# Storing the last four slabs of a 90-degree rotation in 16 KB instead of 8 KB packets

## The chip, the cores and the metric

One core of one Trainium2 chip. The metric is device time in microseconds (us), the median of several executions. A profile's span is the part of it between the first and the last instruction that the profile shows; it is about 1.8 us shorter than the time.

A ratio of two kernels is the mean time of one kernel's fast runs over the mean of the other's fast runs of the same rounds, so it is not quite the ratio of the medians quoted beside it.

## The reference

```python
def setup_inputs():
    batch, c, h, w = 32, 3, 256, 256
    return {"x": np.random.randn(batch, c, h, w).astype(np.float32)}

def reference(x):
    return np.rot90(x, k=-1, axes=(-2, -1)).astype(np.float32)
```

There are 96 images of 256 x 256 fp32 values, each turned by 90 degrees. That is 25.17 MB in and 25.17 MB out, without arithmetic.

## The kernel before

The images are handled in 12 slabs of 8 images, 2 MiB each. A slab is a tile of 128 partitions with 2 x 2048 values. VectorE turns it with two transposes of 128x2048 (STREAM_TRANSPOSE in the trace, 3.83 to 3.95 us each in the means of the page's groups); the rest of the rotation lies in the access patterns. With a right result a slab has long contiguous rows on one side only: if a partition holds 16 rows of the input (16 KB) it ends with twice 8 rows of the output (8 KB), or the other way round.

Before the change, slabs 1 to 8 are loaded in 16 KB rows and slabs 0, 9, 10 and 11 ("plain") in 8 KB rows. All are stored in 8 KB rows. Every DMA is issued from one engine, SyncE. A DMA of 1 MiB is spread over 16 DMA engines, and each row is one packet: the page's 5888 packets are 5248 rows (128 of slab 1, stored in two pieces, count twice) and 40 x 16 completion packets.

```python
    plain = (0, last - 2, last - 1, last)
    # ... views of the rows of x and out: ld8_v, st_v in 8 rows, ld16_v in 16 rows ...
    for n in range(n_slabs):
        for i in range(I):                                   # I = 2
            if n in plain:
                nc.sync.dma_start(out=units[n][:, i], in_=ld8_v[n][:, i])
            else:
                nc.sync.dma_start(out=units[n][i::I].rearrange("p i f -> p (i f)"), in_=ld16_v[n, i])

    for n in range(n_slabs):
        t_in, t_out = units[n], units[n - 1] if n else turned0        # turned0 lies in PSUM
        if n in plain:
            for i in range(I):
                src = t_in[:, i].rearrange("p (r g c) -> p c r g", r=RO, c=RO)
                dst = t_out[:, i].rearrange("p (c g r) -> p c r g", c=RO, r=RO)
                nc.vector.transpose(out=dst[:, :, ::-1, ::-1], in_=src)
        else:
            # ... two transposes, one per half of the rows of out ...
        # slab 1 is stored in three transfers, slabs 2 and 3 in two, the others in one:
        # ...
        elif n:
            nc.sync.dma_start(out=st_v[n], in_=t_out)

    for i in range(I):
        nc.scalar.copy(out=units[last][:, i], in_=turned0[:, i])
    nc.sync.dma_start(out=st_v[0], in_=units[last])
```

Slab n is turned into the tile that slab n - 1 came from; slab 0 waits in PSUM, and ScalarE copies it out at the end. So the order of stores is slab 1, 2, ... 11, and then 0.

## Time and profile before

| | before |
|---|---|
| time, median of 3 | 123.53 us (123.49 to 123.58) |
| span | 121.8 us |
| VectorE busy | 92.7 us, 76% |
| DMA packets, share of 16 engines | 5888, 98.1% |

The first line is the chain of work that ended last, by engine; then come the costliest groups: line, engine, operation, target and source, count, busy time in us, mean ns of one, and the idle time before them.

```profile
DVE 41%; issue 33%; DMA 4%; DVEq 3%; ACT 2%
...
L80 DVE STREAM_TRANSPOSE u<-u 128x2048 f32<-128x2048 f32 x16 | 62.4, 3945 | 0.3
L74 DVE STREAM_TRANSPOSE u<-u 128x2048 f32<-128x2048 f32 x6 | 22.8, 3931 | 0.0
L74 DVE STREAM_TRANSPOSE turned<-u 128x2048 f32<-128x2048 f32 x2 | 7.6, 3828 | 5.6 <-DMA u<-in_x_dram 5.6
```

VectorE (DVE) heads the chain and has almost no idle time once it has started. Both look like a bound.

### The profile page before, as it was taken

Reading aid. Unit: us, or ns where it says so; the run is one execution under the profiler, and the core shown is the slowest. Engines: PE = TensorE matmul, PEld = TensorE weight load, DVE = VectorE, ACT = ScalarE, POOL = GpSimd, SP = SyncE. Lnnn points to the kernel's source line nnn. Section 1 sums busy time; section 2 is a strip of 40 time slices with the busy share of each in tenths; the row PEclk is TensorE's granted clock in tenths of the full one; section 3 lists DMA queues with packets and bytes.
Section 4 is the critical chain, followed back from the end, with each engine's and each line's share of the span. In section 5 each row is a group of like instructions: output and inputs, shape, how many; then the busy total and the mean of one; then the engine's idle time right before and its main releaser. Section 6 shows DMA issues by size and latency. Waiting matters only on the chain.

```text
span 121.8 us, 140 instructions
## 1 busy us (share of the span) xinstructions
DVE 92.7 (76%) x24; ACT 5.0 (4%) x3; POOL 0.2 (0%) x4
## 2 busy tenths in 40 slices
DVE  0199999999999999999999999999999930000000
ACT  0000000000000000000300000000000660000000
POOL 0000000000000000000000000000000000000000
DMA  3999999999999999999999999999999999999995
GB/s 86 425 436 430 430 430 430 430 430 430 430 430 430 430 430 403 430 422 420 420 397 429 430 425 425 430 425 430 428 430 430 428 430 430 425 425 428 425 430 218
DMA packets 5888, 50.33 MB, mean 413 GB/s; under 512 B 640, under 2 KB 768, under 8 KB 896
## 3 DMA queue, kind: packets, MB, share of 16 engines
q1 hardware_dynamic: 5888, 50.33, 98.1%
HBM read 25.17 MB, written 25.17 MB: 413 GB/s over the span
## 4 chain that ended last, share of the span: by engine, by line
DVE 41%; issue 33%; DMA 4%; DVEq 3%; ACT 2%
DVE u L80 31%; DVE turned L74 6%; DMA u<-in_x_dram 4%; DVE u L74 4%; DVEq L120 3%; ACT u L93 2%
## 5 line engine op out<-in xcount | busy, mean ns | idle before, releaser
L80 DVE STREAM_TRANSPOSE u<-u 128x2048 f32<-128x2048 f32 x16 | 62.4, 3945 | 0.3
L74 DVE STREAM_TRANSPOSE u<-u 128x2048 f32<-128x2048 f32 x6 | 22.8, 3931 | 0.0
L74 DVE STREAM_TRANSPOSE turned<-u 128x2048 f32<-128x2048 f32 x2 | 7.6, 3828 | 5.6 <-DMA u<-in_x_dram 5.6
L93 ACT COPY u<-turned 128x2048 f32<-128x2048 f32 x2 | 3.7, 1865 | 35.8 <-DVE u L74 35.8
L93 ACT ACT_TABLE_LOAD x1 | 1.3, 1283 | 59.7 <-DMA u<-in_x_dram 59.7
L109 POOL MEMSET const-bfloat16-1.0<- 128x1 bf16 x1 | 0.1, 101 | 0.0
L109 POOL MEMSET const-uint8-127<- 128x1 uint8 x1 | 0.1, 101 | 0.0
L109 POOL MEMSET const-float32-0.0<- 128x1 f32 x1 | 0.1, 98 | 0.2 <-issue 0.2
L109 POOL MEMSET const-float32-1.0<- 128x1 f32 x1 | 0.1, 98 | 0.0
## 6 DMA issues: line engine op xcount, KB each, us to landing
u<-in_x_dram SPq DMA_DIRECT2D x24, 1024.0 KB, 19.6
out_dram<-u SPq DMA_DIRECT2D x9, 2048.0 KB, 22.8
out_dram<-u SPq DMA_DIRECT2D x5, 1024.0 KB, 17.4
out_dram<-u SPq DMA_DIRECT2D x1, 896.0 KB, 17.5
out_dram<-u SPq DMA_DIRECT2D x1, 128.0 KB, 18.0
```

The costliest lines, as they stand in the source:

```text
L74: nc.vector.transpose(out=dst[:, :, ::-1, ::-1], in_=src)
L80: nc.vector.transpose(out=dst[:, cs], in_=src[:, cs])
L93: nc.scalar.copy(out=units[last][:, i], in_=turned0[:, i])
L109: nc = _bacc.Bacc("TRN2", target_bir_lowering=False, num_devices=1)
L120: with _tile.TileContext(nc) as tc:
```

## The change

Its intent is fewer and longer packets in the stores. The four slabs that are loaded in 8 KB rows are turned the other way, so that a partition holds 16 rows of out, and are stored as two transfers of 64 rows of 16 KB each. To keep the number of transfers, two slabs are loaded, and two stored, in one transfer instead of two.

```diff
     for n in range(n_slabs):
+        if n in (last - 2, last - 1):
+            ld = nc.sync.dma_start(out=units[n], in_=ld_short[n])
+            continue
# ... cut ...
+    def store(n, t, i):
+        if n in long_st:
+            return nc.sync.dma_start(out=st_long[n, i], in_=t[i::I].rearrange("p i f -> p (i f)"))
+        return nc.sync.dma_start(out=st_short[n][:, i], in_=t[:, i])
# ... cut ...
-        if n in plain:
-            for i in range(I):
-                src = t_in[:, i].rearrange("p (r g c) -> p c r g", r=RO, c=RO)
-                dst = t_out[:, i].rearrange("p (c g r) -> p c r g", c=RO, r=RO)
-                nc.vector.transpose(out=dst[:, :, ::-1, ::-1], in_=src)
+        if n in long_st:
+            src = t_in.rearrange("p i (r g c) -> p c r g i", r=RS, c=RL)
+            dst = t_out.rearrange("p i f -> p (i f)").rearrange("p (c k r) -> p c r k", c=RL, r=RS)[:, :, ::-1, ::-1]
+            pieces = 2
+            for h in range(pieces):
+                cs = slice(h * RL // pieces, (h + 1) * RL // pieces)
+                nc.vector.transpose(out=dst[:, cs], in_=src[:, cs])
# ... cut: slabs 2 and 3 stored in one transfer each, slabs 9 to 11 in two each ...
-    nc.sync.dma_start(out=st_v[0], in_=units[last])
+    for i in range(I):
+        store(0, units[last], i)
```

More of the change, by code (lines that the diff above doesn't have):

```diff
@@ L40, with short, long @@
     P = nc.NUM_PARTITIONS
-    RI, RO = 16, 8
-    K = H // RI
+    RL, RS = 16, 8
     I = 2
-    Q = P // (K * I)
+    Q = P * RS // H
     n_slabs = B * C // (Q * I)
     last = n_slabs - 1
-    plain = (0, last - 2, last - 1, last)
-    F = RO * W
+    F = RS * W
+    long_st = (0, last - 2, last - 1, last)
     rows_in = x.rearrange("b c h w -> (b c h) w")
     rows_out = out.rearrange("b c h w -> (b c h) w")
-    ld8_v = rows_in.rearrange("(n i p r) w -> n p i (r w)", i=I, p=P, r=RO)
-    ld16_v = rows_in.rearrange("(n i m r) w -> n i m (r w)", i=I, m=Q * K, r=RI)
-    st_v = rows_out.rearrange("(n i p c) w -> n p i (c w)", i=I, p=P, c=RO)
+    def short(rows):
+        return rows.rearrange("(n i p r) w -> n p i (r w)", i=I, p=P, r=RS)
+    def long(rows):
+        return rows.rearrange("(n i m r) w -> n i m (r w)", i=I, m=P // I, r=RL)
+    ld_short, ld_long, st_short, st_long = short(rows_in), long(rows_in), short(rows_out), long(rows_out)
     pools = [ctx.enter_context(tc.tile_pool(name=f"unit{u}", bufs=1)) for u in range(n_slabs)]
@@ L61 @@
     for n in range(n_slabs):
+        if n in (last - 2, last - 1):
+            ld = nc.sync.dma_start(out=units[n], in_=ld_short[n])
+            continue
         for i in range(I):
-            if n in plain:
-                nc.sync.dma_start(out=units[n][:, i], in_=ld8_v[n][:, i])
-            else:
-                nc.sync.dma_start(out=units[n][i::I].rearrange("p i f -> p (i f)"), in_=ld16_v[n, i])
+            if n in long_st:
+                ld = nc.sync.dma_start(out=units[n][:, i], in_=ld_short[n][:, i])
+            else:
+                ld = nc.sync.dma_start(out=units[n][i::I].rearrange("p i f -> p (i f)"), in_=ld_long[n, i])
@@ L68 @@
+    def store(n, t, i):
+        if n in long_st:
+            return nc.sync.dma_start(out=st_long[n, i], in_=t[i::I].rearrange("p i f -> p (i f)"))
+        return nc.sync.dma_start(out=st_short[n][:, i], in_=t[:, i])
     for n in range(n_slabs):
         t_in, t_out = units[n], units[n - 1] if n else turned0
-        if n in plain:
-            for i in range(I):
-                src = t_in[:, i].rearrange("p (r g c) -> p c r g", r=RO, c=RO)
-                dst = t_out[:, i].rearrange("p (c g r) -> p c r g", c=RO, r=RO)
-                nc.vector.transpose(out=dst[:, :, ::-1, ::-1], in_=src)
-        else:
-            src = t_in.rearrange("p i f -> p (i f)").rearrange("p (r g c) -> p c r g", r=RI, c=RO)
-            dst = t_out.rearrange("p i (c k r) -> p c r k i", c=RO, r=RI)[:, :, ::-1, ::-1, :]
-            for h in range(2):
-                cs = slice(h * RO // 2, (h + 1) * RO // 2)
-                nc.vector.transpose(out=dst[:, cs], in_=src[:, cs])
@@ L82 @@
-        if n == 1:
-            nc.sync.dma_start(out=st_v[n][:, 0, :W], in_=t_out[:, 0, :W])
-            nc.sync.dma_start(out=st_v[n][:, 0, W:], in_=t_out[:, 0, W:])
-            nc.sync.dma_start(out=st_v[n][:, 1], in_=t_out[:, 1])
-        elif n in (2, 3):
-            for i in range(I):
-                nc.sync.dma_start(out=st_v[n][:, i], in_=t_out[:, i])
-        elif n:
-            nc.sync.dma_start(out=st_v[n], in_=t_out)
+        if n in long_st:
+            src = t_in.rearrange("p i (r g c) -> p c r g i", r=RS, c=RL)
[4 more added lines that the diff above has]
+                nc.vector.transpose(out=dst[:, cs], in_=src[:, cs])
+        else:
+            src = t_in.rearrange("p i f -> p (i f)").rearrange("p (r g c) -> p c r g", r=RL, c=RS)
+            dst = t_out.rearrange("p i (c k r) -> p c r k i", c=RS, r=RL)[:, :, ::-1, ::-1, :]
+            for h in range(2):
+                cs = slice(h * RS // 2, (h + 1) * RS // 2)
+                nc.vector.transpose(out=dst[:, cs], in_=src[:, cs])
@@ L92 @@
+        if n in range(2, last - 2):
+            nc.sync.dma_start(out=st_short[n], in_=t_out)
+        elif n:
+            for i in range(I):
+                if (n, i) == (1, 0):
+                    nc.sync.dma_start(out=st_short[n][:, 0, :W], in_=t_out[:, 0, :W])
+                    nc.sync.dma_start(out=st_short[n][:, 0, W:], in_=t_out[:, 0, W:])
+                else:
+                    store(n, t_out, i)
     for i in range(I):
         nc.scalar.copy(out=units[last][:, i], in_=turned0[:, i])
-    nc.sync.dma_start(out=st_v[0], in_=units[last])
+    for i in range(I):
+        store(0, units[last], i)
```

## The prediction

> **What bounds the kernel now.** I read the page's strips by fortieths first, because 50 MB of traffic for 25 MB of input suggests a copy limit. The DMA strip has to be read against the engines' strip:
>
> ```profile
> span 121.8 us, 140 instructions
> DVE 92.7 (76%) x24; ACT 5.0 (4%) x3; POOL 0.2 (0%) x4
> ...
> DMA  3999999999999999999999999999999999999995
> GB/s 86 425 436 430 430 430 430 430 430 430 430 430 430 430 430 403 430 422 420 420 397 429 430 425 425 430 425 430 428 430 430 428 430 430 425 425 428 425 430 218
> DMA packets 5888, 50.33 MB, mean 413 GB/s; under 512 B 640, under 2 KB 768, under 8 KB 896
> ## 3 DMA queue, kind: packets, MB, share of 16 engines
> q1 hardware_dynamic: 5888, 50.33, 98.1%
> ```
>
> The 16 DMA engines are busy in every slice but the first and the last, 98.1% over the span, and the rate is flat near 428 GB/s. VectorE ends around slice 32. So the transfers are the bound: 50.33 MB at 428 GB/s is 117.6 us; the other 4 us are the start (first packet 1.75 us into the span, by the packet records), the slower first packets and the end.
>
> The "chain that ended last" names DVE for 41% and "issue" for 33%, and would mislead here: it follows instructions, and its last one is a copy on ScalarE that ends at 100.5 us, 21 us before the end. What comes after is only the queue. The view of the last store's line shows it:
>
> ```profile
> L94 SPq DMA_DIRECT2D out_dram<-u x1: 373/373/373, 100.5 to 100.5; - x1
> ...
> DMA to landing us min/median/max: 20.5/20.5/20.5
> ```
>
> It is issued at 100.5 us and lands 20.5 us later, at 121.0. Its own 2 MB take 4.9 us at 428 GB/s; the other 15.6 us it stood behind stores issued before it. That is the slack of everything upstream at the end of the run.
>
> Then the windows view, for three stretches of one kind of packet each (start:end, length, busy time of DVE, ACT and POOL, PEclk, DMA share, GB/s), and the DMA view of two of them:
>
> ```profile
> 8.00:42.00 34.00, 33.86 (x10) 0.00 (x0) 0.00 (x0) 1.00 1.01 431
> 48.00:58.00 10.00, 9.97 (x4) 0.00 (x0) 0.00 (x0) 1.00 1.01 422
> 64.00:111.00 47.00, 34.53 (x10) 3.73 (x2) 0.00 (x0) 1.00 1.01 428
> ```
> ```profile
> DMA packets 1119, 14.66 MB, mean 431 GB/s; under 512 B 224, under 2 KB 224, under 8 KB 224
> ...
> q1 hardware_dynamic: 1119, 14.66, 101.1%
> ```
> ```profile
> DMA packets 2662, 20.12 MB, mean 428 GB/s; under 512 B 206, under 2 KB 206, under 8 KB 209
> ...
> q1 hardware_dynamic: 2662, 20.12, 101.2%
> ```
>
> 8 to 42 us is loads in 16 KB packets, 48 to 58 us loads in 8 KB packets, 64 to 111 us stores in 8 KB packets. A 16 KB packet takes (1.011 x 16 x 34 us - 224 completion packets x 9 ns) / 895 = 612 ns; an 8 KB store packet (1.012 x 16 x 47 us - 206 x 9 ns) / 2456 = 309 ns. The packet records give the same medians, 611 and 309 (9 ns for a completion packet). Two 8 KB packets are thus only 6 to 7 ns dearer than one of 16 KB. The packet shares over 100% say that packets of one engine overlap slightly, so these durations overstate spacing.
>
> The cleanest rate is the distance between completions, from the trace's completion records: 2.446 us per MiB for 16 KB loads, 2.486 for 8 KB loads, and 4.895 per 2 MiB, so 2.448 per MiB, for 8 KB stores. **Stores in 8 KB packets already go as fast as loads in 16 KB packets.**
>
> [...]
> - [...] The new stores read even or odd partitions only. [...]the 16 KB loads write just such halves (64 x 4096) at 431 GB/s.
> - [...] The trace's transposes take 3.93 us for 2048 columns, 1.92 ns each, whichever side hops.
>
> **The change part by part.**
> 1. *Stores of slabs 9, 10, 11 and 0*: 4 x 256 packets of 8 KB become 4 x 128 of 16 KB. 512 packets fewer, 32 per DMA engine; total packets 5888 - 512 = 5376. All of it is on the path, since the queue sets the end. By packet duration 32 x 7 ns = 0.22 us. By the loads' own comparison, (2.486 - 2.446) x 8 MiB = 0.32 us. By completions of 16 KB loads against 8 KB stores, (2.448 - 2.446) x 8 = 0.02 us.[...] I choose 0.13 us, between the smallest and the middle, since the stores already run where the 16 KB loads do.
> 2. *Count of transfers*: loads 24 to 22 (slabs 9 and 10 joined), stores 16 to 18 (slabs 2 and 3 joined, the four long ones split). 40 both times, so 640 completion packets and nothing gained or lost. Issue on SyncE is 0.3 to 0.5 us per transfer for 2.4 us of transfer, hidden.
> 3. *First transpose*: it now reads both halves of slab 0, so it waits for the second load too, which lands at 8.06 us instead of 5.57. VectorE, gapless from there (0.3 us of idle before), moves about 2.5 us later and ends near 101.1 instead of 98.6. Both ScalarE copies then come after it: 2 x 1.87 us, so slab 0 is issued near 105 instead of 100.5. Before the change its first byte was due near 121.0 - 4.9 = 116 us. The slack shrinks from 15 to about 10 us; no end moves.
> 4. *The transposes* of the four slabs keep count and size (8 of 128x2048), only source and target order change. I expect 3.8 to 4.0 us each; nothing in the end.
>
> Sum: 123.53 - 0.13 = **123.40 us**.
>
> **The rivals.**
> - *Every packet costs its full overhead[...]*: 0.2 to 0.3 us off, 123.2 to 123.3. For it: the gap between 8 and 16 KB loads, 0.04 us per MiB. Against it: the stores lack that gap already.
> - *VectorE becomes the bound*: the new source order alternates between halves 8 KB apart every element.[...] Against it: the present order hops as much on the target in 16 of 24 transposes at the same 3.95 us.
> - *Strided partitions or 16 KB writes are bad for stores*:[...] A loss of 5% on 8 MiB would be 1.0 us, 124.4. Against it: the loads of this shape.
> - *A coarser tail*: the last completions of the 16 engines lie 0.49 us apart now; with packets twice as long the last could come 0.1 to 0.3 us later and eat the gain: 123.5 to 123.6.
> - *Queue runs dry* where issues wait for earlier completions: at most eight transfers are in flight, and the late ones are now 1 MiB rather than 2. Eight MiB are still 19 us of work. I give it little.
>
> **Range and chances.**[...] 2% would be 2.5 us, so faster by over 2% is nearly excluded: 0.01. Slower by over 2% takes the second or third rival in a strong form: 0.02. Within 2%: 0.97. The times before agree within 0.09 us, so the range is narrow: 123.0 to 123.75, wider above 123.4 for the tail and strided reads.
>
> **What would show it.** 5376 packets and 98% DMA share; the 16 KB stores in the last 20 us at 428 to 433 GB/s, packets near 611 ns; the first transpose near 8.1 us and the last copy ending near 105 us with the DMA strip still at 9 to the end; the last landing near 120.9. The prediction is wrong if the changed transposes take over 4.5 us, if the strip shows a gap after 60 us, or if 16 KB store packets take over 630 ns.

The forecast's sum is 123.53 - 0.13 = 123.40 us, with the 0.13 chosen among 0.02 (completions), 0.22 (packet durations) and 0.32 us (the two kinds of loads). "Nearly excluded" rests on the largest of the three estimates, 0.32 us, against 2.5. The "slower first packets" are 8 KB packets of up to 1285 ns instead of 309 in the first 5 us of the trace before.

## The result, and the profile after

| | before | after |
|---|---|---|
| median | 123.60 us (6 runs, 123.49 to 124.06) | 123.56 us (6 runs, 123.45 to 123.68) |
| ratio | | 0.9992, 95% interval 0.9976 to 1.0009 |
| span | 121.8 us | 121.9 us |
| DMA packets | 5888 | 5376 |

The time is the same. The page after, in the same views as before:

```profile
span 121.9 us, 139 instructions
DVE 92.9 (76%) x24; ACT 4.9 (4%) x3; POOL 0.2 (0%) x4
...
DMA  4999999999999999999999999999999999999994
GB/s 86 427 444 430 430 430 430 430 430 430 425 430 425 430 430 406 417 430 425 398 416 428 427 425 430 430 427 425 427 430 427 427 433 446 430 430 430 430 430 183
DMA packets 5376, 50.33 MB, mean 413 GB/s; under 512 B 640, under 2 KB 768, under 8 KB 896
...
q1 hardware_dynamic: 5376, 50.33, 98.1%
...
DMA 65%; DVE 10%; issue 3%; DVEq 3%; ACT 2%; ACTq 1%; SPq 1%
...
L95 DVE STREAM_TRANSPOSE u<-u 128x2048 f32<-128x2048 f32 x16 | 62.4, 3945 | 0.3
L89 DVE STREAM_TRANSPOSE u<-u 128x2048 f32<-128x2048 f32 x6 | 23.4, 3983 | 0.1
L89 DVE STREAM_TRANSPOSE turned<-u 128x2048 f32<-128x2048 f32 x2 | 7.1, 3586 | 8.2 <-DMA u<-in_x_dram 8.2
```

512 packets are gone, the DMA share and the mean rate are as before, and the strip has no gap. The last seven full slices stand at 430 to 446 GB/s, where before they stood at 425 to 430. The first transpose waits 8.2 us instead of 5.6, because it now reads both halves of slab 0. The chain's line shows how little that view may be trusted here: from 41% DVE it went to 65% DMA, in two kernels that are bound by the same queue. It happened to be followed through the completions this time.

What happened inside is seen in the trace's completion records, that is, when the last of a transfer's 16 DMA engines reports its data landed. I cut the run at four landings that all kernels have: the first load, the 23rd MiB of loads, slab 1's last store, and the last store. The time from the 23rd MiB of loads to slab 1, in which loads hand over to stores, is called the hand-over. Every row of this table is one profiled execution, in us:

| kernel | transfers | first load | 23 MiB loaded | hand-over | slabs 2 to 0 | last landing | from there to the end |
|---|---|---|---|---|---|---|---|
| before | 40 | 5.57 | 59.65 | 7.53 | 53.84 | 121.02 | 0.81 |
| before, again | 40 | 5.64 | 59.68 | 7.72 | 53.84 | 121.24 | 0.82 |
| after | 40 | 5.62 | 59.70 | 7.69 | 53.70 | 121.08 | 0.81 |
| after, again | 40 | 5.62 | 59.67 | 7.75 | 53.67 | 121.10 | 0.81 |
| long stores only | 44 | 5.52 | 59.62 | 7.67 | 53.77 | 121.06 | 1.07 |
| long stores only, 48 | 48 | 5.58 | 59.64 | 7.72 | 53.70 | 121.06 | 0.82 |
| joins only | 36 | 5.65 | 59.70 | 7.59 | 53.84 | 121.14 | 0.99 |
| all loads 16 KB | 40 | 5.98 | 59.78 | 7.88 | 53.83 | 121.49 | 0.82 |
| all stores 16 KB, loads 8 KB | 48 | 5.57 | 60.23 | 7.38 | 53.41 | 121.03 | 0.81 |
| mix | 40 | 5.62 | 59.55 | 7.90 | 53.73 | 121.18 | 0.81 |
| stores 16 KB (wrong result) | 48 | 5.67 | 59.74 | 7.63 | 53.50 | 120.88 | 0.81 |
| stores 4 KB (wrong result) | 40 | 5.65 | 59.67 | 7.78 | 55.14 | 122.60 | 0.81 |
| VectorE 7 us later | 40 | 5.54 | 59.64 | 7.65 | 53.71 | 121.00 | 0.81 |
| VectorE 14 us later | 40 | 5.62 | 59.81 | 7.80 | 59.40 | 127.01 | 0.82 |

The column "slabs 2 to 0" is steady: twice 53.84 for the kernel before, 53.70 and 53.67 for the changed one. So the long stores did save about 0.15 us. The four changed slabs alone, from the landing of slab 8 to the last one, took 19.57 and 19.56 us in the two traces before and 19.46 and 19.45 after, which is 0.11 us less; what is left of the 0.15 lies in slabs whose packets did not change. The hand-over isn't steady: 7.53 and 7.72 for the same kernel. In the first pair of traces it took 0.16 us more after the change and cancelled the gain.

(The expectations below call the 23rd MiB of loads the 22nd; the landing at 59.65 us that they mean is the 23rd.)

### The profile page after: what moved, and what is told of

It is laid out like the page before. It is cut to its first block, busy times and chain, and to the rows that moved or that the text cites. A ratio compares the mean times of both kernels' runs of the same rounds, so it can differ in the third digit from the quotient of the medians.

```text
span 121.9 us, 139 instructions
## 1 busy us (share of the span) xinstructions
DVE 92.9 (76%) x24; ACT 4.9 (4%) x3; POOL 0.2 (0%) x4
## 2 busy tenths in 40 slices
DMA packets 5376, 50.33 MB, mean 413 GB/s; under 512 B 640, under 2 KB 768, under 8 KB 896
## 3 DMA queue, kind: packets, MB, share of 16 engines
q1 hardware_dynamic: 5376, 50.33, 98.1%
## 4 chain that ended last, share of the span: by engine, by line
DMA 65%; DVE 10%; issue 3%; DVEq 3%; ACT 2%; ACTq 1%; SPq 1%
DMA u<-in_x_dram 45%; DMA out_dram<-u 20%; DVE u L89 10%; DVEq L136 3%; ACT u L108 2%; ACTq L136 1%; SPq L72 1%; SPq L74 0%; SPq L98 0%
## 5 line engine op out<-in xcount | busy, mean ns | idle before, releaser
L89 DVE STREAM_TRANSPOSE turned<-u 128x2048 f32<-128x2048 f32 x2 | 7.1, 3586 | 8.2 <-DMA u<-in_x_dram 8.2
```

The costliest lines, as they stand in the source:

```text
L89: nc.vector.transpose(out=dst[:, cs], in_=src[:, cs])
```

## The experiments

The theory was: **the stores gain about 5 ns for each packet saved, which is real and small, and the time hides it under the chance of the hand-over.** Its rivals: the joined transfers gave the gain back; the long packets are worth nothing in stores; VectorE's later start took it.

### One part alone: the long stores, or the joins

Long stores only, against the kernel before (the transposes as in the change):

```diff
# ... cut: the transposes of the four slabs, and the store of slab 0 in two 16 KB transfers, as in the change ...
+        elif n and n in plain:
+            for i in range(I):
+                nc.sync.dma_start(out=st16_v[n, i], in_=t_out[i::I].rearrange("p i f -> p (i f)"))
         elif n:
             nc.sync.dma_start(out=st_v[n], in_=t_out)
```

> The kernel before with only the four long stores (slabs 9, 10, 11 and 0 turned so that a partition holds 16 rows of out and stored in 16 KB packets, two 1 MiB transfers each); its loads stay 24 transfers and slabs 2 and 3 keep two stores each, so 44 transfers. Theory A (packet cost, small): the last 8 MiB of stores complete at 2.430 us per MiB as in the changed kernel, against 2.447 before, so 0.14 us less, of which 4 more completion packets of 9 ns take 0.04 back: ratio to before about 0.999. Rival B (the joined transfers, not the long stores, cost the 0.2 us that the changed kernel lost where loads hand over to stores): here that loss is absent, and slab 8 lands at 101.45 us as before, the last at about 121.3 less 0.45, so 120.9. Rival C (the 0.2 us was chance of one execution): the landing of slab 8 scatters by 0.2 us from run to run, whatever the kernel.

Measured: 123.98 us, ratio 1.0015 (1.0001 to 1.0029). Slabs 2 to 0 took 53.77 us, and the four changed slabs 19.46 us as in the changed kernel, so the gain was there. The last store landed at 121.06. But the run ended 1.07 us later instead of 0.81, which no theory had foreseen.

Joins only:

```diff
+        if n in (last - 2, last - 1):
+            nc.sync.dma_start(out=units[n], in_=ld8_v[n])
+            continue
# ... and slabs 2 and 3 stored by the line for the others
-        elif n in (2, 3):
-            for i in range(I):
-                nc.sync.dma_start(out=st_v[n][:, i], in_=t_out[:, i])
```

> The kernel before with only the joins: slabs 9 and 10 loaded in one 2 MiB transfer each, slabs 2 and 3 stored in one each; stores all in 8 KB packets, 36 transfers. Theory A: 4 completion packets fewer, 0.04 us less, ratio 1.000. Rival B (the joins cost 0.2 us at the hand-over from loads to stores): slab 8 lands near 101.65 us instead of 101.45, and the last at 121.2 instead of 121.0, ratio 1.0015. Rival C: anything within 0.2 us of before.

Measured: 124.03 us, ratio 1.0020 (1.0008 to 1.0032). The hand-over was 7.59 us, between the two of the kernel before. The other traces agree: both loads joined (after, joins only and VectorE later) 7.59 to 7.80 us, no load joined 7.38 to 7.90. So the joins do not make that loss: rival B falls. Here too the end came late, 0.99 us after the last landing.

Each part alone was timed 0.2 us slower than before, and both together were not. The instructions after the last landing show a part of this. SyncE closes the program by checking the eight completion semaphores of its transfers in a fixed order. Transfers take the eight in turn. With 40 transfers the last one signals a semaphore that is checked at the end (before, that check starts at 121.04 us, after the last landing at 121.02, and the first drain at 121.11); with 44 or 36 it is one that is checked near the beginning, and the other checks, already fulfilled, still follow, some 62 ns apart in the trace. To test it, the long-stores kernel was given four transfers more:

```diff
-        elif n in (2, 3):
+        elif n in range(2, 8):
```

> The long-stores-only kernel again (44 transfers, right result, 1.07 us from the last landing to the end), with slabs 4 to 7 also stored in two transfers each: 48, a multiple of the 8 completion semaphores. Theory F (the closing checks walk the semaphores in a fixed order, about 62 ns each, and with 44 or 36 transfers the last landing is on the fourth from the end, so four or so more checks come after it): 0.81 us from the last landing to the end, as in the kernel before, 0.25 us less than with 44, although there are four transfers more. Rival (the 0.2 us belongs to the long stores or to the number of transfers): 1.07 us or more. Slabs 2 to 0 take 53.75 us (53.69 in the changed kernel, and 6 x 9 ns). Timed: within chance of before, 0.998 to 1.001.

Measured: 0.82 us from the last landing to the end instead of 1.07, in both cases with the last landing at 121.06. SyncE's drains, which follow the checks, in the views of the closing line, with count, min/median/max ns, and first and last start (first 44 transfers, then 48):

```profile
L126 SPq DRAIN x3: 7/7/13, 121.4 to 121.7; - x3
```
```profile
L126 SPq DRAIN x3: 7/7/13, 121.1 to 121.4; - x3
```

The first drain moves from 121.4 to 121.1 us under the same landing: theory F holds. The joins of the change keep the count at 40, and in the trace this is what they are worth. The timed ratio does not follow, though: 1.0024 (1.0010 to 1.0038), 124.02 us. The mean span of the timed runs is 121.98 us, as good as the 121.97 of the kernel before, but the part of the time outside the span is 2.06 us instead of 1.79. The two other kernels with 48 transfers show 1.94 and 1.97. What this part consists of no view shows; it is left open. So the closing checks fit the longer mean spans with 44 and 36 transfers (122.13 and 122.22 us), and no gain in time from 48 is shown.

### Chance: both kernels a second time

> The changed kernel once more, unaltered, for a second trace and a narrower interval. All theories: ratio 0.999 with an interval of about 0.15%. Rival C (chance) expects the landing of slab 8 to differ from the first trace's 101.63 us by 0.1 us or more and the last 8 MiB again to take 19.45 us, 2.43 per MiB; rival B (joins) expects 101.6 again.

> The kernel before, unaltered, for a second trace of it and for the size of chance. Theory E (the loss of 0.1 to 0.3 us at the hand-over from loads to stores is chance of the execution, for the DMA engines leave it 0.5 to 0.85 us apart in the traces so far): from the landing of the 22nd MiB of loads (59.65 us in the first trace) to that of slab 8 it took 41.80 us; this time it differs by 0.1 us or more. Rival B (the changed kernel's order of transfers makes the loss): 41.80 again within 0.05 us, where the changed kernel twice had 41.93 and 41.98. Timed ratio 1.000 with an interval of 0.15%.

Measured: the changed kernel 123.71 us, ratio 0.9999 (0.9980 to 1.0017). The kernel before, 123.58 us against 123.78 for its twin, ratio 0.9980 with an interval of 0.9964 to 0.9995. **Two identical programs differ by 0.2% here, and the interval excludes 1.** No difference of 0.2 us can be settled by the timed ratios.

The traces separate the two effects. The hand-over of the kernel before took 7.53 us the first time and 7.72 the second, a difference of 0.19 (theory E), with the changed kernel's 7.69 and 7.75 next to the second. The packet records show where the time goes: between 60.3 and 61.0 us of the first trace twelve of the last packets of the loads start that take 471 to 581 ns instead of 309, and the first packets of the stores start at 61.3. How far apart this leaves the DMA engines differs from run to run: on slab 1 the first and the last of the 16 engines to land lie 0.48 us apart in one trace of the kernel before and 0.84 us in the other, and the distance stays to the end. What slows these packets was not examined. Nor are two sources of the scatter told apart: these calls ran on different chips (11, 14 and 1; the record names none for the first two traces), and on each of the three the hand-overs of different kernels lie 0.27 to 0.42 us apart. Set beside each other, the second traces show 121.24 us for the last landing before and 121.10 after, which is the gain of the stores.

### What a packet costs: all stores longer, or shorter

The change touches 8 of 24 MiB. Two kernels with a wrong result (the rows go to wrong places) change 22 MiB, with transposes as before, and loads too but for slab 10 of the first kernel, which is loaded in one transfer:

```diff
# ... cut: the load of slab 10; slabs 2, 3 and 0 stored the same way ...
-            nc.sync.dma_start(out=st_v[n], in_=t_out)
+            for i in range(I):
+                nc.sync.dma_start(out=st16_v[n, i], in_=t_out[i::I].rearrange("p i f -> p (i f)"))
```
```diff
+    st4_v = rows_out.rearrange("(n i p r) w -> n p i (r w)", i=2 * I, p=P, r=RO // 2)
# ... cut: slabs 2, 3 and 0 stored the same way ...
-            nc.sync.dma_start(out=st_v[n], in_=t_out)
+            nc.sync.dma_start(out=st4_v[n], in_=t_out.rearrange("p i (a f) -> p (i a) f", a=2))
```

> Wrong result on purpose: the kernel before with its own loads and transposes, but slabs 2 to 11 and 0 stored in 16 KB packets, 22 MiB instead of the change's 8; slab 10 is loaded in one transfer so that the count of transfers is 48, a multiple of 8 as in the kernel before (40). Theory A (a packet saved is worth 5 ns: 8 MiB saved 0.12 us in three traces, plus 4 x 9 ns of added completion packets, over 32 packets per DMA engine): the landings of slabs 2 to 0 take 22 x 2.431 = 53.5 us instead of 53.84, so 0.35 us less; ratio 0.997 give or take the hand-over. Rival (7 ns, from the packet durations of 611 and 309 ns): 0.5 us less. Rival (no gain at all in stores): 53.84.

> Wrong result on purpose: the kernel before with slabs 2 to 11 and 0 stored in 4 KB packets, otherwise the same transfers (40). 22 MiB x 8 = 176 packets more per DMA engine. Theory A (5 ns a packet): the landings of slabs 2 to 0 take 53.84 + 0.88 = 54.7 us, ratio 1.007. Rival (7 ns): 55.1 us, ratio 1.010. Rival (10 ns, what 8 KB loads cost against 16 KB loads): 55.6 us, ratio 1.014.

The DMA views of the stretch from 70 to 117 us, all of it stores (packets, bytes and rate), in the order 16, 8 (the kernel before) and 4 KB:

```profile
DMA packets 1537, 20.20 MB, mean 430 GB/s; under 512 B 304, under 2 KB 304, under 8 KB 304
```
```profile
DMA packets 2631, 20.11 MB, mean 428 GB/s; under 512 B 176, under 2 KB 176, under 8 KB 176
```
```profile
DMA packets 4948, 19.58 MB, mean 416 GB/s; under 512 B 169, under 2 KB 169, under 8 KB 4948
```

Halving the packet from 8 to 4 KB takes 12 GB/s; doubling it gives 2. Measured by landings, slabs 2 to 0 took 53.50, 53.84 and 55.14 us. A completion packet costs 9 ns (the median of its records in the traces of both kernels), and the kernels have 22, 13 and 13 transfers there:

- 16 against 8 KB: (0.34 us + 9 x 9 ns) for 88 packets saved on each DMA engine, 4.8 ns a packet. The change itself: (0.155 us + 2 x 9 ns) for 32 packets, 5.4 ns; by its four slabs alone, which have four transfers more, (0.11 us + 4 x 9 ns), 4.6 ns.
- 4 against 8 KB: 1.30 us for 176 packets more, 7.4 ns a packet on average.

So doubling the packets of stores saves what theory A says, 5 ns each, and the rivals of 7 ns and of nothing fall there. For 4 KB packets the total is what the rival of 7 ns said (55.1 us), and theory A's 54.7 is too low. But this total joins two different stretches of one trace. Slabs 2 to 8 took 34.88 us against 34.27, which is 5.4 ns for each of 112 packets more; slabs 9 to 0 took 20.26 against 19.57, 10.8 ns for each of 64. The windows show the step (start:end, length, busy time of DVE, ACT and POOL, PEclk, DMA share, GB/s), first with 4 KB packets, then in the kernel before:

```profile
70.00:98.00 28.00, 27.97 (x8) 1.87 (x1) 0.00 (x0) 1.00 1.02 421
100.00:117.00 17.00, 0.00 (x0) 0.60 (x1) 0.00 (x0) 1.00 1.02 409
```
```profile
70.00:98.00 28.00, 27.96 (x8) 1.86 (x1) 0.00 (x0) 1.00 1.01 428
100.00:117.00 17.00, 0.00 (x0) 0.50 (x1) 0.00 (x0) 1.00 1.01 428
```

The median 4 KB packet takes 159 ns in the first window and 164 in the second. VectorE ends near 99 us in both kernels, and the 8 KB stores keep their rate, so that alone is no cause; it stays open. Up to there theory A's 5 ns holds for 4 KB packets too, and the agreement of the total with 7 ns is luck. That a packet's cost depends on its size is not shown.

Timed: 123.65 us and 0.9982 (0.9966 to 0.9997) for 16 KB, 125.29 us and 1.0115 (1.0096 to 1.0133) for 4 KB. The wrong results carry over to time as far as the rows have the same lengths and number as in a right program of that packet size.

### The opposite choice, and the choice carried to all slabs

If the long side of a slab is to be chosen, which side gains more? All slabs loaded in 16 KB rows and stored in 8 KB rows:

```diff
-    plain = (0, last - 2, last - 1, last)
+    plain = ()
```

> The opposite choice for the same four slabs: the kernel before with slabs 0, 9, 10 and 11 also loaded in 16 KB packets (64 x 4096) and stored in 8 KB packets; right result. Theory A (loads gain more from long packets than stores): by completions 8 KB loads take 2.486 us per MiB and 16 KB loads 2.446, so 8 MiB save 0.32 us, against 0.14 for the long stores: ratio 0.9974, 123.25 us. Rival (per packet cost is the same for loads and stores, 4 to 7 ns): 0.13 to 0.22 us, ratio 0.9985. Rival D (the first slab's 8 KB loads matter for an early first transpose): the first transpose starts at 8.1 instead of 5.6 us, no effect on the end.

Measured: 124.15 us, ratio 1.0032 (1.0020 to 1.0045), slower, where theory A had expected 0.3% less. The loads did gain: from the first landing to the 23rd MiB it took 53.80 us instead of 54.08, 0.28 less for the 6 MiB between these landings that changed, where 0.24 was expected. But the first load landed at 5.98 instead of 5.57 us: its first packet started at 2.08 us into the span instead of 1.75, by the packet records. And the hand-over was 7.88 us, the last loads' packets now taking up to 1131 ns instead of 611; but 7.90 occurs with 8 KB loads too (the mix below), so a loss there by the longer packets is not shown. The step that fell is the silent assumption that the start stays as it is. The page's line for the loads shows the start, transfers issued from 0.7 us on, and the shortest time to landing:

```profile
L66 SPq DMA_DIRECT2D u<-in_x_dram x24: 471/472/612, 0.7 to 42.7; - x24
...
DMA to landing us min/median/max: 5.3/19.6/20.0
```

The same view of the kernel before, for the 8 KB loads, has 4.8.

```profile
L64 SPq DMA_DIRECT2D u<-in_x_dram x8: 328/331/422, 0.7 to 42.3; - x8
...
DMA to landing us min/median/max: 4.8/19.7/19.9
```

The change carried to all slabs, right result:

```diff
-    long_st = (0, last - 2, last - 1, last)
+    long_st = range(n_slabs)
# ... and every slab loaded, and stored, in two transfers
```

> The change carried to all slabs, right result: every slab loaded in 8 KB packets, turned so that a partition holds 16 rows of out, and stored in 16 KB packets, 48 transfers. Theory A (loads lose 0.040 us per MiB, stores gain 0.015): the first 22 MiB of loads land 0.64 us later than in the changed kernel, at 60.3 us; slabs 2 to 0 take 53.50 us as in the run with all stores long, 0.2 less than in the changed kernel; together 0.3 to 0.4 us more than the changed kernel, ratio to before 1.002. Rival (long packets are worth as much in stores as in loads): no change against the kernel before.

Measured: 123.87 us, ratio 1.0014 (0.9995 to 1.0033), of which the part outside the span makes 0.18 us. By phases the loads landed 0.53 us later than in the changed kernel (60.23 against 59.70), and slabs 2 to 0 took 0.29 less (53.41). The hand-over came out at 7.38 us, the shortest of all. This kernel does not split slab 1's first 1 KB off, which by packet times (8 x (46 + 272 - 309) ns and one completion) is worth 0.08 us, and it stores slab 1 in long packets, some 0.03; the rest lies in the range of chance. So the last landing, 121.03, is level with the changed kernel's, not 0.3 later as theory A had it in total. Its terms for loads and stores came out (0.53 where 0.64 was expected, 0.29 where 0.2 was); the sum is within the hand-over's chance.

A candidate for the best of both: slab 0 in 8 KB loads for an early start, slab 11 in 8 KB loads before the hand-over, the others in 16 KB loads.

```diff
-    plain = (0, last - 2, last - 1, last)
+    plain = (0, last)
# ... slabs 0 and 11 turned and stored as in the change, 2 and 3 stored in one transfer each, the others as in the kernel before
```

> A candidate to beat both, right result, 40 transfers: slab 0 (for an early start) and slab 11 (last before the hand-over) loaded in 8 KB and stored in 16 KB packets, all other slabs loaded in 16 KB and stored in 8 KB. By landings: loads of slabs 9 and 10 save 4 MiB x 0.04 = 0.16 us against before, stores of slabs 11 and 0 save 4 x 0.015 = 0.06 us: ratio to before 0.998, to the changed kernel 0.999. Theory E: the hand-over adds or takes 0.15 us by chance, so one trace may hide it.

Measured: 123.91 us, ratio 1.0003 (0.9986 to 1.0021). It led by 0.10 to 0.15 us at the 23rd MiB (59.55), and the slowest hand-over of all, 7.90, took it away. It is not a gain that can be shown. No version beats both kernels clear of chance.

### How far VectorE is from the path

The changed kernel, with slab 0 turned two or three times over:

```diff
-            for h in range(pieces):
+            for h in list(range(pieces)) * (2 if n == 0 else 1):     # 3 in the second kernel
```

> The changed kernel with its first slab turned twice over (2 transposes more, 7.2 us of VectorE work in front of everything). Theory A (VectorE is off the path, with slack): its last transpose ends at 101.5 + 7.2 = 108.7 us, the store of slab 11 is issued then and its first packet would come 1.0 us later, at 109.7, before the queue is empty at about 111.0: no change, the last landing near 121.1. Rival (the page's chain is right and VectorE carries the end): 7.2 us more.

> The changed kernel with its first slab turned three times (4 transposes more, 14.4 us). Theory A with the slack worked out: last transpose at 115.9 us, first packet of slab 11 at 116.9, the queue empty from about 111.0: a gap of 5.9 us, and the end 5.7 to 5.9 us later, ratio 1.047. Rival 1 (VectorE carries the end already): 14.4 us more, ratio 1.117. Rival 2 (VectorE is irrelevant however late): no change.

Measured: 123.78 us, ratio 1.0008 (0.9987 to 1.0029), and 129.57 us, ratio 1.0472 (1.0454 to 1.0489). With 7 us more of VectorE work nothing happens, with 14 us the end comes 5.9 us later, as worked out. The strips of the second kernel, in 40 slices of 3.2 us:

```profile
span 127.8 us, 143 instructions
DVE 106.8 (84%) x28; ACT 4.9 (4%) x3; POOL 0.2 (0%) x4
...
DMA  3999999999999999999999999999999990955995
GB/s 105 418 456 426 420 436 441 420 426 436 441 415 431 431 408 420 423 418 423 382 423 436 418 441 418 433 423 431 431 418 443 431 420 41 410 246 246 410 410 246
```

The DMA strip has holes now, 0 and 5, each time the queue has stored one slab and waits for the next. The total was foreseen, the picture not: I had one gap in mind, and there are two, 2.7 us before slab 10 and 3.0 us before slab 11 by their landings, since VectorE makes a slab in 7.9 us and the queue stores one in 4.9. A 1 MiB store that finds the queue empty lands 4.2 us after its issue (115.53 to 119.71 us). In the changed kernel the same store landed at 113.80 behind others, so it might have been issued as late as 109.6; it was issued at 101.55. The slack is 8.1 us.

## Why the prediction was right

It said 123.40 us, 123.0 to 123.75, and within 2% with 0.97; measured were 123.56 us and 0.9992, and 123.71 us and 0.9999. The range would have held an unchanged kernel too, so the time alone says nothing of the mechanism; the traces do.

- **The bound.** Right. 98.1% DMA share before and after, and the chain's DVE share is no bound: VectorE could be 7 us later for nothing.
- **Step 1, the packets.** Right in mechanism and, by landings, in size: 0.13 us chosen, 0.14 to 0.17 measured in slabs 2 to 0 and 0.11 in the four changed slabs alone. That the choice came so near is partly luck, for it was a middle taken between estimates of 0.02 and 0.32. The packets number 5376, and the 16 KB stores landed at 2.431 us per MiB (19.45 us for 8 MiB, 431 GB/s) with a median packet of 611 ns. The argument in which the stores' gain was feared to be 0.02 us, because 8 KB stores already run like 16 KB loads, failed: stores of 16 KB took 2.431 us per MiB and loads of 16 KB 2.446, so loads were no measure for stores here. The packet duration, 7 ns, was too high as a price, as the overlap named there suggested; some 5 ns is what the landings give.
- **Step 2, the count of transfers.** "Nothing gained or lost" holds for 40 and 40, but the prediction did not see what the count protects: 44 or 36 cost 0.17 to 0.25 us of closing checks in the traces. Issuing took longer than its 0.3 to 0.5 us, up to 1.37 us for a long store, and stayed hidden.
- **Step 3, the first transpose.** Right: it starts at 8.22 us, the last one ends at 101.52 (101.1 foretold), and slab 0 is issued at 105.2. The slack of "about 10 us" was read off slab 0; the store that binds first is that of slab 11, with 8.1.
- **Step 4, the transposes.** 3.98 us in SBUF, within 3.8 to 4.0. The two into PSUM fell from 3.83 to 3.59, faster than I had allowed.
- **The rivals.** VectorE did not become the bound (7 us more of its work gave 123.78 us, ratio 1.0008), reading every second partition cost nothing (430 GB/s from 70 to 117 us in the wrong-result kernel with 16 KB stores from 64 x 4096, 428 before), and no coarser tail can be seen: the last landings of the 16 engines lay 0.62 and 0.79 us apart after the change, 0.49 and 0.80 before.
- **What was missing.** The chance of the hand-over, 0.2 us between two runs of the same kernel, is larger than the gain. In the first pair of traces it is the reason that the last landing came at 121.08 us and not near 120.9 as foretold. In the timed runs, which scatter as widely, the gain cannot be seen: it is shown by the traces alone.

## What to carry to other kernels

In a kernel at 98% DMA share, price a change of packet size by the number of packets per DMA engine times the cost of one (some 5 ns here) before writing it, and see whether that exceeds the run-to-run chance. Time the unchanged kernel as if it were a new one: here that gave 0.2%, more than the change itself moved. Where a difference is smaller than that, cut the trace at landings that both kernels have and compare the steady stretch alone, in several pieces, since a total can hide a step within it; and look at what follows the last landing, where the mere number of transfers was worth 0.25 us in the trace.
